# Weight rests moved from GpSimd to VectorE, a scaling moved from VectorE to ScalarE, and more PSUM banks for the output projection

## The chip, the cores and the metric

The kernel runs on one core of a Trainium2 chip. The core has TensorE (matrix products, results in PSUM), VectorE, ScalarE and GpSimd (elementwise work), and SyncE, which issues most of the transfers. Each engine works through its own instructions strictly in order and waits at semaphores for the others. The metric is the device time of one execution in microseconds (us); lower is better.

## The reference

One decoder layer over two token groups: a prompt of 512 tokens with 16 meta tokens ahead of it, and 64 sample tokens (8 sequences of 8). All is float32.

```python
u = rmsnorm(h, norm1_w)
z, xbc, dt_raw, q, k, v, qi, ki, wi, g_ssm, g_attn = split_in(u @ w_in)
y_ssm, ssm_new, conv_new = ssm_mixer(z, xbc, dt_raw, conv_prefix, h0, segments, ...)
y_att = attend(q, k, v, qi, wi, ki)        # indexer picks top-k keys, softmax over these
merged = sigmoid(g_ssm) * (y_ssm @ w_ssm_proj) + sigmoid(g_attn) * (y_att @ w_attn_proj)
h = h + merged @ w_out
u2 = rmsnorm(h, norm2_w)
h = h + square(relu(u2 @ w_up)) @ w_down
y = rmsnorm(h, final_norm_w)
```

The widths are 1024 for the model, 9320 for `w_in`, 2048 for the state-space branch and 4096 for the feed-forward part.

## The kernel before

**Three products for one.** Each large product in float32 precision is made of three on TensorE. An operand x is split into a head (x rounded to the fp32r format) and a rest (x minus its head); then head·head, head·rest and rest·head are added up in PSUM. For weights `weights` (L125) does this for each block of 128 x 1024 elements (512 KB): SyncE loads it into `wr` (2 buffers), ScalarE writes the head `wh` (L122), and GpSimd writes the rest `wl` by a subtraction (L123, in `split`). For `w_out` and `w_down` the two are called `dh` and `dl` (7 buffers each); for the others `wh` and `wl` (3 each). `wr` comes free for the next load when the rest is written. One first block has its rest on VectorE already. `split` also makes the rest `kL` of the indexer's keys, and `ysl` of the state-space outputs, which takes GpSimd and VectorE in turn.

**Stages, in order of time.** Norm and transposes; the indexer with its top-k (L420, L421 for the prompt, L529, L530 for the samples: a max and a replace in turn, on VectorE); the input projection, tile by tile (`mm3`, L145), whose tiles go through a convolution (`conv_tile`: L582 three times for one tile, then L587); the state-space scan (`states`, `chunk`), which is interleaved with the convolution by a small pipeline; the gates; the sample attention; the prompt's sparse attention (`query`) beside the projection of the state-space branch (L1039); the attention projection (L145 again, then L1072, L1073 and L1076 on VectorE); the output projection (`add_product`, L1164, called at L1185); and the feed-forward part in eight steps (`up` for w_up, `add_product` for w_down).

**In the scan** a chunk masks eight heads on VectorE (L733, tile `bc`) and feeds each to TensorE (L734). GpSimd weighs inputs (L665, L645), scales states (L678, L759), adds (L762, L766, L767) and takes powers (L155); L775 then writes a diagonal `rd` on VectorE for TensorE (L778).

**In the prompt's attention** `query` computes scores on TensorE, adds the mask with VectorE (L975), takes the exponential on ScalarE (L978), divides by the sum by means of a VectorE multiplication in place (L989, tile `P2`), and transposes on TensorE (L995).

**In the output projection** each `add_product` makes two halves of 512 columns; each half takes one PSUM bank of the tag "s" (3 banks), gets 8 or 12 products, and is added to `h2` by VectorE (L1178). Tag "a" has 3 banks too (used by `up` and, in turn with tag "w", by the transposes of the second norm); tag "w" has 2.

**What sets the order.** The program is written without engine queues: a scheduler works out the order of each engine's instructions ahead of time from dependencies, free buffers and its own cost figures. So a change of engine moves other instructions too. At run time the order of each engine is fixed.

Of the kernel before, what the change touches and what calls it, by code (L numbers as in the profile page):

```python
# [9 lines left out]
FT = mybir.dt.float32  # L10
# [3 lines left out]
AF = mybir.ActivationFunctionType  # L14
OP = mybir.AluOpType
# [55 lines left out]
def body(ctx, tc, a, o):  # L71
    nc = tc.nc
    SB, PS, DR = bass.MemoryType.SB, bass.MemoryType.PSUM, bass.MemoryType.DRAM
    act, dve, pool, pe, sy = nc.scalar, nc.vector, nc.gpsimd, nc.tensor, nc.sync
# [9 lines left out]
    def pst(tag):  # L84
        return psp.tile([128, 512], FT, tag=tag, name=tag, bufs=PSB[tag])
# [18 lines left out]
    def mis():  # L104
        alt[0] += 1
        return pst("as"[alt[0] % 2])

    def flat(t):
        return t.rearrange("p a b -> p (a b)")
# [10 lines left out]

    def split(raw, hi, lo, lo_eng=None):
        act.activation(hi, raw, AF.Copy)  # L122
        (lo_eng or pool).tensor_tensor(lo, raw, hi.bitcast(FT), op=OP.subtract)  # L123

    def weights(parts, at=None, lo_eng=None):  # L125
        raw = wp.tile([128, 8, 128], FT, tag="wr", name="wr", bufs=WB[0])
        lo, hi = [(at[0] if at else wp).tile([128, 8, 128], FR, tag=n, name=n, bufs=at[2] if at else WB[1])
                  for n in (at[1] if at else ("wl", "wh"))]
        for sel, src in parts:
            sy.dma_start(sel(raw), src)  # L130
        split(raw, hi, lo, lo_eng)
        return hi, lo
# [65 lines left out]
    for t in range(5):  # L198
# [7 lines left out]
        for q in range(2):  # L206
            ps = mis()
            pv = ps.rearrange("p (k n) -> p k n", k=4)
            for i in range(4):
                k = 4 * q + i  # L210
# [9 lines left out]
    ps = mis()  # L220
# [4 lines left out]
    ps = mis()  # L225
# [4 lines left out]
    for q in range(2):  # L230
        ps = mis()
# [23 lines left out]
    def inproj(parts, n=HT, w=None):  # L255
        w = w or weights(parts)
        out = []
        for h in range(2):
            ps = pst("w")
            mm3(ps, w, uh, ul, h * n, h * n + n)  # L260
            out.append(ps)
        return out

    def in_cols(c0):
        return [(lambda r: r, block(w_in, 0, c0))]
# [22 lines left out]
    with tc.tile_pool(name="p1", bufs=1) as p1:  # L288
# [11 lines left out]
        ps = mis()  # L300
# [4 lines left out]
        ps = mis()  # L305
# [10 lines left out]
        for ct in range(4):  # L316
            ps = inproj(in_cols(C_QI + 128 * ct) if ct else None, n=HQ, w=None if ct else wq0)
# [7 lines left out]
        kS = p1.tile([128, 528], FR, name="kS")  # L325
        kL = p1.tile([128, 528], FR, name="kL")
        split(kiT[:, 0:528], kS, kL)


# [15 lines left out]
        for t in range(4):  # L345
            L = LT[t]
            sc = am[:, LO[t]:LO[t] + L]
            for h in range(8):
                lq = qS[:, h, 128 * t:128 * t + 128]
                r = p1.tile([128, 528], FT, tag="ri", name="ri", bufs=2)  # L350
                for c0, c1 in pieces(L):
                    ps = mis()
# [20 lines left out]
        ps = mis()  # L373
# [34 lines left out]
        for c0, c1 in pieces(1032):  # L408
            ps = pst("a")
# [41 lines left out]
        ps = mis()  # L451
# [10 lines left out]
        ps = mis()  # L462
# [3 lines left out]
        ps = mis()  # L466
# [5 lines left out]
        ps = mis()  # L472
# [8 lines left out]
        ps = mis()  # L481
# [5 lines left out]
        ps = mis()  # L487
# [13 lines left out]
        for kt in range(6):  # L501
            c0, n = ((128 * kt, 128) if kt < 4 else (512, 16) if kt == 4 else (528, 64))
            ps = pst("s")
# [10 lines left out]
        for kp in range(8):  # L514
            hp, gi = divmod(kp, 4)
            parts = []
            for e in range(2):
                c0 = C_Q + 64 * (8 * hp + 4 * e + gi)
                parts.append((lambda r, e=e: r[:, :, 64 * e:64 * e + 64],
                              w_in[:, c0:c0 + 64].rearrange("(k p) c -> p k c", p=128)))  # L520
            ps = inproj(parts, n=HQ)
# [393 lines left out]
    with tc.tile_pool(name="p2h", bufs=1, reuse_waits="tile", side="right") as p2h, \  # L915
# [6 lines left out]
        for kv in range(4):  # L922
            hp, e = divmod(kv, 2)
# [13 lines left out]
        def query(t, hp, gp):  # L937

            L, nk = LT[t], t + 1
# [23 lines left out]
            cuts = [(0, L)] if L <= 512 else [(0, 400), (400, L)]  # L963
            PT = p2.tile([128, 2, 4, 2, 128], FT, tag="PT", name="PT", bufs=2)
            PR = p2.tile([96, 256], FR, tag="PR", name="PR", bufs=2)
            for g in range(2):
                P2 = p2q.tile([128, 2, 528], FT, tag="P", name="P2", bufs=3)
                mx = p2q.tile([128, 2, 6], FT, tag="mx", name="mx", bufs=4)
                for e in range(2):
                    lq = QS[:, 2 * gp + g, e, :]  # L970
                    for i, (c0, c1) in enumerate(cuts):
                        v = pst("s")[:, :c1 - c0]
                        pe.matmul(v, lq, KS[:, 2 * hp + e, c0:c1], start=True, stop=False)
                        pe.matmul(v, lq, KL[:, 2 * hp + e, c0:c1], start=False, stop=True)
                        dve.tensor_tensor_reduce(P2[:, e, c0:c1], v, at[:, c0:c1], 1.0, NEG, OP.add, OP.max,  # L975
                                                 accum_out=mx[:, e, i:i + 1])
                    dve.tensor_scalar(mx[:, e, 2:3], mx[:, e, 0:1], mx[:, e, len(cuts) - 1:len(cuts)], -0.125, op0=OP.max, op1=OP.mult)
                    act.activation(P2[:, e, :L], P2[:, e, :L], AF.Exp, scale=0.125, bias=mx[:, e, 2:3],  # L978
                                   accum_out=mx[:, e, 3:4])
                dve.reciprocal(mx[:, :, 4:5], mx[:, :, 3:4])  # L980
                tl = p2q.tile([128, 32], FT, tag="tl", name="tl", bufs=3)
                tv = tl.rearrange("p (e n) -> p e n", e=2)
                pool.tensor_tensor(tv, P2[:, :, 128 * nk:L], mx[:, :, 4:5].to_broadcast([128, 2, 16]), op=OP.mult)
                ts = p2q.tile([128, 3, 32], FR, tag="ts", name="ts", bufs=3)
                for i in range(2):
                    pool.tensor_copy(ts[:, i, :], tl)
                pool.tensor_tensor(ts[:, 2, :], tl, ts[:, 0, :].bitcast(FT), op=OP.subtract)
                for e in range(2):
                    dve.tensor_scalar(P2[:, e, :128 * nk], P2[:, e, :128 * nk], mx[:, e, 4:5], None, op0=OP.mult)  # L989
                yield  # L990
                for e in range(2):
                    ps = pst("a")
                    pv = ps.rearrange("p (k n) -> p k n", k=4)
                    for j in range(nk):
                        pe.transpose(pv[:, j, :], P2[:, e, 128 * j:128 * j + 128], idf)  # L995
                    (act.copy if e else dve.tensor_copy)(PT[:, e, :nk, g, :], pv[:, :nk, :])
                pr_ = pst("a")
                pe.transpose(pr_[:96, 0:128], flat(ts).bitcast(FT), idf)
                act.copy(PR[:, 128 * g:128 * g + 128], pr_[:96, 0:128])
# [11 lines left out]
            dve.tensor_tensor(yal[:, k0:k0 + 2, 128 * t:128 * t + 128], pv, h_.bitcast(FT), op=OP.subtract)  # L1011

        Pipe().run(query(t, hp, gp) for t in range(4) for hp in range(2) for gp in range(2))

    HALVES = ((0, HQ), (HQ, NQ))
    PARTS = ((0, 256), (256, NQ))
    w_s, w_a = a["w_ssm_proj"][0], a["w_attn_proj"][0]
    for q in range(4):
# [7 lines left out]
        for m in range(8):  # L1026
# [8 lines left out]
            for c0, c1 in HALVES:  # L1035
                ps = pst("w")
# [14 lines left out]
    mgh = p4a.tile([128, 8, NQ + NS], FR, name="mgh")  # L1051
    mgl = p4a.tile([128, 8, NP], FR, name="mgl")
# [5 lines left out]
    for m in range(8):  # L1058
# [9 lines left out]
        for c0, c1 in HALVES:  # L1068
            ps = pst("w")
# [19 lines left out]
    def row_weights(src, r0, n, at=(p4w, ("dl", "dh"), 7)):  # L1089

        return [[flat(x) for x in weights([(flat, src[r0 + 128 * k:r0 + 128 * k + 128, :])], at)] for k in range(n)]
# [25 lines left out]
    nb = [0]  # L1117

    def norm2(t):
        src, r = row_norm(t, t)  # L1120
        n = 128 if t < 4 else 64
        xn = p4.tile([128, D], FT, tag="jk", name="xn2", bufs=2)[:n]
        dve.scalar_tensor_tensor(xn, src, r, wrow[:n], op0=OP.mult, op1=OP.mult)
        if t == 4:
            pool.memset(h2[64:128, 4, :], 0.0)
        return lambda: turn2(t, xn, n)
# [34 lines left out]

    PIECES = ((0, 512), (512, 768), (768, 1024))

    def add_product(t, xh, xl, ws, cuts=((0, 512), (512, 1024))):  # L1164

        tok = slice(128 * t, 128 * t + 128)
        for c0, c1 in cuts:
            cc = slice(c0, c1)
            ps = pst("s")[:, :c1 - c0]
            for k, (wh, wl) in enumerate(ws):  # L1170
                if t < 4:
                    terms = (xh[k][:, tok], wh), (xl[k][:, tok], wh), (xh[k][:, tok], wl)
                else:
                    terms = (xh[k][:, tok], wh), (xh[k][:, tok], wl)
                for i, (x, w) in enumerate(terms):
                    pe.matmul(ps, x, w[:, cc], start=(k == 0 and i == 0),  # L1176
                              stop=(k == len(ws) - 1 and i == len(terms) - 1))
            dve.tensor_tensor(h2[:, t, cc], h2[:, t, cc], ps, op=OP.add)  # L1178
# [3 lines left out]
    for q in range(2):  # L1182
        ws = row_weights(a["w_out"][0], 512, 4) if q else wo
        for t in ORDER:
            add_product(t, [mgh[:, 4 * q + k, :] for k in range(4)], [mgl[:, 4 * q + k, :] for k in range(4)], ws)  # L1185
            if q == 1:
                turns.append(norm2(t))
                if t in (0, 1, 2):
                    turns.pop(0)()
# [40 lines left out]
    for s in range(8):  # L1230
        ws = [] if s < 7 else row_weights(a["w_down"][0], 512 * s, 4)
        nxt = ups(s + 1, ws) if s < 7 else None
        for i, t in enumerate(ORDER):
            add_product(t, *prev, ws, **({"cuts": PIECES} if s == 7 and i == 4 else {}))
            if s == 7 and i > 0:
                final(ORDER[i - 1])
        prev = nxt
# [26 lines left out]
```

## Time and profile before

| | |
|---|---|
| median of 3 runs | 1539.23 us (1535.28 to 1539.56) |
| the profiled execution | 1540.31 us |
| its span, first to last instruction | 1538.5 us |
| mean TensorE clock in it, share of full speed | 0.981 |

The profile gives for each engine the time in which it ran an instruction, as a share of the span, and for each group of instructions the count, busy time and mean. "Idle before, and its releaser" is the time the engine stood still just ahead of an instruction and what ended that. In a row of the view of waits, the engine on the left waited for the one on the right: total in us, how often, the longest. Rows of a timeline give the start in us, how long, engine, line, operation, output <- inputs. PE is TensorE's products, PEld its weight loads, DVE VectorE, ACT ScalarE, POOL GpSimd. Products overlap in TensorE's pipeline, so that a row of 0.30 us does not mean that the next one starts 0.30 us later.

### The profile page before, as it was taken

To read this page: it belongs to the slowest core of one execution; us is meant where nothing else is said; L and a number is where in the kernel's file an instruction comes from. 1 tells how busy PE (TensorE), PEld (TensorE's weight loads), DVE (VectorE), ACT (ScalarE), POOL (GpSimd) and SP (SyncE) were. 2 spreads that over 40 slices of the span, in tenths; PEclk is the share of its full clock that TensorE was granted. 3 is DMA by queue.
4 is the path that set the end of the run, shared out by engine and by line. 5 is a ranking of instruction groups with operands and counts; after the bars stand their busy time and mean duration, and the time that the engine had idled before them with its cause. 6 is when DMAs were issued, how large, how long until landed. Compare 5 with 4: busy or idle time off the path is not lost.

```text
span 1538.5 us, 26571 instructions
## 1 busy us (share of the span) xinstructions
PE 1456.4 (95%) x9960; PEld 1304.1 (85%) x9960; DVE 1008.7 (66%) x1905; ACT 667.8 (43%) x1484; POOL 713.8 (46%) x644
## 2 busy tenths in 40 slices
PE   6899999899998998999999999989998999999998
PEld 5888989898887987989678988888897998899886
DVE  5799999769769677363533788764565644564444
ACT  4454444555665654343645665522342321232211
POOL 2422353656666657465444964344154533352322
PEclk9999999999999999999999999999999999999999
DMA  6424645677886977766964532135233312332212
GB/s 173 115 56 107 171 141 149 204 232 204 231 238 169 261 209 208 210 180 202 339 218 145 154 90 80 33 119 183 58 98 108 110 55 69 96 95 68 71 41 69
DMA packets 297609, 221.55 MB, mean 144 GB/s; under 512 B 43820, under 2 KB 267360, under 8 KB 297456
## 3 DMA queue, kind: packets, MB, share of 16 engines
q1 hardware_dynamic: 292232, 200.98, 45.9%
q0 software_dynamic: 5248, 18.88, 3.6%
q8 instruction: 78, 1.28, 0.4%
q14 instruction: 51, 0.42, 0.1%
HBM read 174.97 MB, written 44.07 MB: 142 GB/s over the span
## 4 chain that ended last, share of the span: by engine, by line
PE 63%; DVE 16%; DMA 8%; issue 5%; ACT 4%; POOL 3%; SPq 2%; POOLq 0%; DVEq 0%; ACTq 0%
PE w L145 16%; PE s L1176 15%; PE a L145 10%; PE w L1039 7%; DVE ca L582 3%; PE s L871 2%; DVE bc L733 2%; DVE scs L530 2%; DMA bc<-d_ac 1%; DVE m8s L529 1%; ACT wh L122 1%; POOL wl L123 1%; DVE r L1200 1%; PE s L1005 1%; DMA wr<-in_w_up_dram 1%
## 5 line engine op out<-in xcount | busy, mean ns | idle before, releaser
L123 POOL TENSOR_TENSOR wl<-wr,wh 128x1024 fp32r<-128x1024 f32 x128 | 310.3, 2424 | 348.7 <-ACT wh L122 333.8
L145 PE MATMUL w<-uh,wh 128*128 128x288 f32 (+1 forms) x1168 | 359.6, 308 | 13.7 <-ACT rb L566 4.8
L145 PE MATMUL w<-ul,wh 128*128 128x288 f32 (+1 forms) x1168 | 358.0, 307 | 0.6 <-DVE ul L214 0.6
L145 PE MATMUL w<-uh,wl 128*128 128x288 f32 (+1 forms) x1168 | 356.3, 305 | 0.0
L145 PEld LDWEIGHTS w<-uh,wh 128*128 128x128 f32 x1168 | 226.3, 194 | 18.5 <-ACT rb L566 6.0
L145 PEld LDWEIGHTS w<-ul,wh 128*128 128x128 f32 x1168 | 226.2, 194 | 3.8 <-issue 2.3
L145 PEld LDWEIGHTS w<-uh,wl 128*128 128x128 f32 x1168 | 225.1, 193 | 2.9 <-issue 2.4
L122 ACT ACTIVATE wh<-wr 128x1024 fp32r<-128x1024 f32 x129 | 136.2, 1056 | 107.7 <-PE w L145 52.0
L123 POOL TENSOR_TENSOR dl<-wr,dh 128x1024 fp32r<-128x1024 f32 x40 | 99.1, 2480 | 157.9 <-ACT dh L122 157.9
L145 PE MATMUL a<-u2h,wh 128*128 128x288 f32 (+2 forms) x512 | 151.5, 296 | 1.0 <-ACT r L1199 1.0
L145 PE MATMUL a<-u2l,wh 128*128 128x288 f32 (+2 forms) x512 | 151.2, 296 | 0.0
L145 PE MATMUL a<-u2h,wl 128*128 128x288 f32 (+2 forms) x512 | 151.1, 295 | 0.0
L1178 DVE TENSOR_TENSOR h<-h,s 128x512 f32<-128x512 f32 (+1 forms) x101 | 67.1, 678 | 125.1 <-PE s L1176 124.5
L1176 PE MATMUL s<-dh,hh 128*128 128x512 f32 (+1 forms) x324 | 128.1, 396 | 6.2 <-DVE h L1178 6.2
L1176 PE MATMUL s<-dl,hh 128*128 128x512 f32 (+1 forms) x324 | 127.5, 395 | 0.0
L582 DVE SCALAR_TENSOR_TENSOR ca<-rb,cwT,ca 128x616 f32<-128x616 f32 x72 | 103.4, 1436 | 15.1 <-ACT ca L580 14.2
L1200 DVE TENSOR_TENSOR r<-r 128x288 f32<-128x288 f32 (+2 forms) x64 | 74.3, 1161 | 53.3 <-ACT r L1199 53.3
L122 ACT ACTIVATE dh<-wr 128x1024 fp32r<-128x1024 f32 x40 | 42.3, 1059 | 152.5 <-PE s L1176 131.2
L1176 PE MATMUL s<-dh,hl 128*128 128x512 f32 (+1 forms) x260 | 102.7, 395 | 0.0
L145 PEld LDWEIGHTS a<-u2h,wh 128*128 128x128 f32 x512 | 96.0, 188 | 2.1 <-ACT r L1199 1.5
L145 PEld LDWEIGHTS a<-u2l,wh 128*128 128x128 f32 x512 | 96.1, 188 | 0.7
L145 PEld LDWEIGHTS a<-u2h,wl 128*128 128x128 f32 x512 | 96.0, 188 | 0.0
(378 smaller groups left out, 3313.9 us busy)
## 6 DMA issues: line engine op xcount, KB each, us to landing
wr<-in_w_in_dram SPq DMA_DIRECT2D x64, 512.0 KB
wr<-in_w_up_dram SPq DMA_DIRECT2D x32, 512.0 KB
wr<-in_w_down_dram SPq DMA_DIRECT2D x32, 512.0 KB
st<-in_state_ssm_dram SPq DMA_DIRECT2D x16, 512.0 KB
bc<-d_ac SPq DMA_DIRECT2D x32, 256.0 KB
out_dram<-st SPq DMA_DIRECT2D x16, 512.0 KB
wr<-in_w_ssm_proj_dram SPq DMA_DIRECT2D x16, 512.0 KB
d_xd<-th SPq DMA_DIRECT2D x16, 296.0 KB
```

The source lines that it names most:

```text
L122: act.activation(hi, raw, AF.Copy)
L123: (lo_eng or pool).tensor_tensor(lo, raw, hi.bitcast(FT), op=OP.subtract)
L145: pe.matmul(ps[:, :c1 - c0], p[:, k, :], x[:, c0:c1], start=(k == 0 and i == 0), stop=(k == 7 and i == 2))
L529: dve.max(m8, scs)
L530: dve.match_replace(scs, m8, scs, MARK)
L582: dve.scalar_tensor_tensor(ca[:, 0:616], rb[:, k:k + 616], cwT[:, 24 * k + ct:24 * k + ct + 1], ca[:, 0:616], op0=OP.mult, op1=OP.add)
L733: dve.scalar_tensor_tensor(mt, mt, dts[:n, c, 8 * g + hh:8 * g + hh + 1], cb[:n, :n], op0=OP.mult, op1=OP.mult)
L871: pe.matmul(v[64 * hp:64 * hp + 64], QZ[:, hp, :], kk, start=True, stop=True)
L1039: pe.matmul(ps[:, :HQ], p[:, k, mc], x[k][:, c0:c1], start=(k == 0 and i == 0), stop=(k == 3 and i == 2))
L1176: pe.matmul(ps, x, w[:, cc], start=(k == 0 and i == 0), stop=(k == len(ws) - 1 and i == len(terms) - 1))
L1178: dve.tensor_tensor(h2[:, t, cc], h2[:, t, cc], ps, op=OP.add)
L1200: dve.tensor_tensor(r, r, r, op=OP.mult)
```

## The change

Three edits. The default engine of the subtraction in `split` becomes VectorE, which moves the rests of all weight blocks and of `kL`. The scaling of the prompt's probabilities goes to ScalarE as a copy with a scale per row. The output projection takes its PSUM banks in turn from the tags "s" and "a", six in all; `add_product` for w_down stays with "s".

```diff
     def split(raw, hi, lo, lo_eng=None):
         act.activation(hi, raw, AF.Copy)
-        (lo_eng or pool).tensor_tensor(lo, raw, hi.bitcast(FT), op=OP.subtract)
+        (lo_eng or dve).tensor_tensor(lo, raw, hi.bitcast(FT), op=OP.subtract)
...
                 for e in range(2):
-                    dve.tensor_scalar(P2[:, e, :128 * nk], P2[:, e, :128 * nk], mx[:, e, 4:5], None, op0=OP.mult)
+                    act.activation(P2[:, e, :128 * nk], P2[:, e, :128 * nk], AF.Copy, scale=mx[:, e, 4:5])
...
-    def add_product(t, xh, xl, ws, cuts=((0, 512), (512, 1024))):
+    def add_product(t, xh, xl, ws, cuts=((0, 512), (512, 1024)), banks="s"):
...
-            ps = pst("s")[:, :c1 - c0]
+            nb[0] += 1
+            ps = pst(banks[nb[0] % len(banks)])[:, :c1 - c0]
...
-            add_product(t, [mgh[:, 4 * q + k, :] for k in range(4)], [mgl[:, 4 * q + k, :] for k in range(4)], ws)
+            add_product(t, [mgh[:, 4 * q + k, :] for k in range(4)], [mgl[:, 4 * q + k, :] for k in range(4)], ws, banks="sa")
```

The lines behind L1168 move down by one. The order changes on all engines; three places show how.

GpSimd in the scan, second group of heads, third chunk of the prompt, before (xw, xb, hn, y, ss are tiles of the scan, rb of the convolution):

```order
L665 TENSOR_TENSOR xw<-xt,wdt 128x512
L645 TENSOR_TENSOR xb<-xb,wds 96x512
L759 TENSOR_TENSOR hn<-hn,elast 128x512
L563 MEMSET rb 128x3
L565 COPY rb<-scT 128x8x3
L155 TENSOR_TENSOR ss<-ss,cst 128x1
L123 TENSOR_TENSOR wl<-wr,wh 128x1024
L762 TENSOR_TENSOR y_5716<-y_5716,xd 128x512
```

The same place after the change:

```order
L665 TENSOR_TENSOR xw<-xt,wdt 128x512
L635 TENSOR_TENSOR xt_5858<-xt_5858,wdt 16x512
L759 TENSOR_TENSOR hn<-hn,elast 128x512
L645 TENSOR_TENSOR xb<-xb,wds 96x512
L762 TENSOR_TENSOR y_5716<-y_5716,xd 128x512
```

The weight's rest is gone from the run of GpSimd instructions; the scan's own have stayed, in a slightly other order.

VectorE in the scan, first group of heads, ahead of a chunk's masks, before:

```order
L728 TENSOR_TENSOR cb<-a,cst 128x128
L582 SCALAR_TENSOR_TENSOR ca<-rb,cwT,ca 128x616
L733 SCALAR_TENSOR_TENSOR bc<-bc,dts,cb 128x128 x8
L582 SCALAR_TENSOR_TENSOR ca<-rb,cwT,ca 128x616
L775 TENSOR_SCALAR rd<-cst,ss 128x128
```

The same chunk after the change:

```order
L728 TENSOR_TENSOR cb<-a,cst 128x128
L123 TENSOR_TENSOR wl<-wr,wh 128x1024
L733 SCALAR_TENSOR_TENSOR bc<-bc,dts,cb 128x128 x3
L587 SCALAR_TENSOR_TENSOR rb<-th,ca 128x528
L590 SCALAR_TENSOR_TENSOR rb<-th,ca 128x64
L733 SCALAR_TENSOR_TENSOR bc<-bc,dts,cb 128x128 x5
```

A weight's rest now stands in VectorE's queue ahead of the masks that TensorE waits for.

VectorE in the attention projection, in the fifth of its eight blocks, before (tga is the gate tile, mgl and mgh the rest and head of the merged activations):

```order
L1072 SCALAR_TENSOR_TENSOR tga<-tga,w 128x288
L1073 TENSOR_TENSOR tga<-tga,ms 128x288
L1076 SCALAR_TENSOR_TENSOR mgl<-tga,mgh 128x224
L1076 SCALAR_TENSOR_TENSOR mgh<-tga,mgh 128x64
L1072 SCALAR_TENSOR_TENSOR tga<-tga,w 128x288
```

The same place after the change:

```order
L1072 SCALAR_TENSOR_TENSOR tga<-tga,w 128x288
L123 TENSOR_TENSOR dl<-wr,dh 128x1024
L1073 TENSOR_TENSOR tga<-tga,ms 128x288
L123 TENSOR_TENSOR wl<-wr,wh 128x1024
L1076 SCALAR_TENSOR_TENSOR mgl<-tga,mgh 128x224
L1076 SCALAR_TENSOR_TENSOR mgh<-tga,mgh 128x64
L1072 SCALAR_TENSOR_TENSOR tga<-tga,w 128x288
```

The rests of `w_out` (dl) and of the projection's blocks (wl) now lie between the steps that free TensorE's banks.

## The prediction

> **What bounds the kernel now.** I read the page's first part, then the chain of waits, then the busy times by stage, then who TensorE waited for.
>
> ```profile
> PE 1456.4 (95%) x9960; PEld 1304.1 (85%) x9960; DVE 1008.7 (66%) x1905; ACT 667.8 (43%) x1484; POOL 713.8 (46%) x644
> ...
> PE 63%; DVE 16%; DMA 8%; issue 5%; ACT 4%; POOL 3%; SPq 2%; POOLq 0%; DVEq 0%; ACTq 0%
> ```
>
> TensorE is the bound: 95% busy, 63% of the chain. GpSimd, which does the work that is moved, holds only 3% of the chain, so its own 46% gives nothing by itself. The second place is VectorE, with 16%. The view by stretches shows where TensorE is not fed:
>
> ```profile
> 37.00:50.00 13.00, 9.20 (x50) 8.85 (x50) 11.57 (x14) 4.53 (x11) 10.27 (x9) 0.74 0.57 148
> 276.00:290.00 14.00, 10.19 (x65) 9.66 (x64) 13.97 (x19) 5.68 (x12) 7.52 (x7) 0.88 0.54 160
> 607.00:622.00 15.00, 8.04 (x45) 7.80 (x44) 10.30 (x6) 4.83 (x10) 12.13 (x10) 0.77 0.63 180
> 1030.00:1046.00 16.00, 11.01 (x67) 10.81 (x66) 9.14 (x9) 5.24 (x7) 7.54 (x4) 0.79 0.32 115
> 1163.00:1178.00 15.00, 10.03 (x36) 7.80 (x35) 8.71 (x11) 6.05 (x9) 9.56 (x4) 0.77 0.42 127
> ...
> 1200.00:1480.00 280.00, 279.08 (x1668) 252.47 (x1667) 149.98 (x166) 79.93 (x138) 107.55 (x44) 1.00 0.28 81
> ```
>
> After the length of the stretch stand PE, PEld, DVE, ACT and POOL busy, then the granted clock. In most of the feed-forward part (1200 to 1480) TensorE stands still for 0.9 of 280 us: nothing to gain there. The five short stretches each hold a hole of 4 to 7 us, and behind it a clock below 1. With half speed as the lower step, a mean clock of 0.79 over 16 us means 2 x 0.21 x 16 = 6.7 us at half speed, and a loss of half of that. The five hold 6.8 + 3.4 + 6.9 + 6.7 + 6.9 = 30.7 us at half speed, a loss of 15.4.
>
> Who ended TensorE's holes (total, count, longest):
>
> ```profile
> PE s L734 <- DVE bc L733: 9.8, 5, 4.2
> ...
> PE a L778 <- DVE rd L775: 7.0, 1, 7.0
> PE w L145 <- DVE tga L1072: 5.2, 2, 5.0
> ...
> PE a L602 <- DVE rb L587: 4.2, 4, 2.5
> PE w L145 <- DVE qS L322: 3.2, 1, 3.2
> ```
>
> and in the stretch from 1000 to 1172:
>
> ```profile
> PE s L1176 <- DVE h L1178: 7.1, 4, 5.0
> ```
>
> That is 36.5 us, all behind VectorE. The timeline says why VectorE was late (DVE and POOL rows of the same moments):
>
> ```profile
> 489.56 6.40 DVE L733 SCALAR_TENSOR_TENSOR bc<-bc,dts,cb 128x128 f32<-128x128 f32 x2
> 492.26 2.33 POOL L123 TENSOR_TENSOR wl<-wr,wh 128x1024 fp32r<-128x1024 f32 x1
> ...
> 608.23 6.89 DVE L775 TENSOR_SCALAR rd<-cst,ss 128x128 f32<-128x128 f32 x1 [1.57 <-POOL ss L155]
> 612.01 2.35 POOL L123 TENSOR_TENSOR wl<-wr,wh 128x1024 fp32r<-128x1024 f32 x1
> ...
> 1033.11 2.31 DVE L1076 SCALAR_TENSOR_TENSOR mgl<-tga,mgh 128x224 fp32r<-128x224 f32 x1 [4.34 <-ACT mgh L1074]
> 1035.35 2.35 DVE L1076 SCALAR_TENSOR_TENSOR mgh<-tga,mgh 128x64 fp32r<-128x64 f32 x1
> 1032.82 4.80 POOL L123 TENSOR_TENSOR dl<-wr,dh 128x1024 fp32r<-128x1024 f32 x2 [6.82 <-ACT dh L122]
> ...
> 1165.87 2.39 DVE L1203 TENSOR_TENSOR hl<-r,hh 128x288 fp32r<-128x288 f32 x1 [1.49 <-ACT hh L1201]
> 1168.18 2.59 DVE L1200 TENSOR_TENSOR r<-r 128x288 f32<-128x288 f32 x1
> 1165.58 2.36 POOL L123 TENSOR_TENSOR wl<-wr,wh 128x1024 fp32r<-128x1024 f32 x1 [2.92 <-ACT wh L122]
> ```
>
> A VectorE instruction that starts while GpSimd writes a rest ends with it: 64 columns take 2.35 us. This is common; three groups, first with their means, then with least, median and longest:
>
> ```profile
> L582 DVE SCALAR_TENSOR_TENSOR ca<-rb,cwT,ca 128x616 f32<-128x616 f32 x72 | 103.4, 1436 | 15.1 <-ACT ca L580 14.2
> ...
> L1200 DVE TENSOR_TENSOR r<-r 128x288 f32<-128x288 f32 x58 | 65.6, 1132 | 46.2 <-ACT r L1199 46.2
> L733 DVE SCALAR_TENSOR_TENSOR bc<-bc,dts,cb 128x128 f32<-128x128 f32 x128 | 62.9, 558 | 0.7 <-ACT xd L765 0.5
> ...
> L582 DVE SCALAR_TENSOR_TENSOR ca<-rb,cwT,ca x72: 834/918/3835, 193.3 to 573.8; 128x616 f32<-128x616 f32 x72
> ...
> L1200 DVE TENSOR_TENSOR r<-r x64: 425/455/2656, 1110.5 to 1479.2; 128x288 f32<-128x288 f32 x58, 128x256 f32<-128x256 f32 x3, 128x320 f32<-128x320 f32 x3
> ...
> L733 DVE SCALAR_TENSOR_TENSOR bc<-bc,dts,cb x160: 267/340/5339, 329.5 to 697.3; 128x128 f32<-128x128 f32 x128, 64x64 f32<-64x64 f32 x32
> ```
>
> Beyond what they need alone these spend (1436-834) x 72 = 43 us, (1132-455) x 58 = 39 and (558-340) x 128 = 28: 110 us.
>
> **The change part by part.** *The rests.*
>
> ```profile
> L123 POOL TENSOR_TENSOR wl<-wr,wh 128x1024 fp32r<-128x1024 f32 x128 | 310.3, 2424 | 348.7 <-ACT wh L122 333.8
> L123 POOL TENSOR_TENSOR dl<-wr,dh 128x1024 fp32r<-128x1024 f32 x40 | 99.1, 2480 | 157.9 <-ACT dh L122 157.9
> ...
> L123 DVE TENSOR_TENSOR wl<-wr,wh x1: 1220/1220/1220, 16.8 to 16.8; 128x1024 fp32r<-128x1024 f32 x1
> ```
>
> GpSimd loses 409 us. VectorE gets 168 x 1.22 = 205 us and gets back the 110 us above and what other groups wasted; so it grows by 95 us at most, with some 530 us idle now. A block's rest is also there 1.2 us sooner, and its load buffer free.
>
> What TensorE gains, hole by hole. Scan masks (9.8): other GpSimd work stands beside the rest, so I count the rest alone, 2.33 in each of the two long holes, 4.7; bounds 0 and 9.8. `rd` (7.0): likewise 2.35; bounds 0 and 7.0. Attention projection (5.2): 2.31 + 2.35 shrink to at most 0.455 each, the median of the wider L1200: 3.75. First product of the feed-forward part (5.0): 2.39 + 2.59 shrink the same way: 4.1. Convolution (4.2): I take 3. First stage (3.2): I take 2; both bounded by 0 and their rows. Sum 20 us. *The clock behind them*: at 37, 276, 1030 and 1163 the hole nearly closes, so 23.8 us at half speed go, worth 11.9; at 607 a hole of over 4 us stays and I count nothing. Sum 31.9.
>
> What it costs. VectorE is full in one stage, the top-k and first convolutions:
>
> ```profile
> 80.00:280.00 200.00, 192.06 (x1368) 181.61 (x1366) 196.64 (x370) 97.43 (x224) 74.61 (x67) 0.99 0.46 126
> 280.00:720.00 440.00, 411.20 (x3139) 372.94 (x3140) 300.75 (x520) 228.85 (x547) 267.61 (x252) 0.97 0.76 212
> 840.00:1000.00 160.00, 158.74 (x1157) 140.11 (x1154) 126.72 (x448) 95.12 (x255) 94.99 (x168) 1.00 0.32 92
> ...
> L123 POOL TENSOR_TENSOR wl<-wr,wh x25: 2359/2399/2812, 84.3 to 278.7; 128x1024 fp32r<-128x1024 f32 x25
> ```
>
> From 80 to 280 it is busy for 196.6 of 200 us, and 25 rests fall there: 25 x 1.22 = 30 us more, some 13 less in L582 (22 of its 72 lie there by start, so 22/72 of 43). The 17 left can slide: the sample top-k isn't needed before the sample attention, and in the new order 8 of its 32 rounds stand ahead of the first finished convolution tile, where 13 stood. From 280 to 720 VectorE has 139 us to spare. I take 5 us lost, of 0 to 17.
>
> The rest brings a wait onto VectorE too: it now waits for ScalarE's head, and so for the load, and behind it in the queue stand L733, L587 and L1073, for which TensorE waits. GpSimd's waits there were
>
> ```profile
> POOL wl L123 <- ACT wh L122: 67.8, 22, 5.5
> ```
>
> (280 to 720). How many of them held work that was ready, the row does not say, and the rests will stand among other work on VectorE. I take 4 us, of 0 to half of the 67.8.
>
> *The scaling.* Alone, ScalarE's copies bound it:
>
> ```profile
> L989 DVE TENSOR_SCALAR P<-P,mx x64: 274/434/1756, 858.6 to 988.2; 128x128 f32<-128x128 f32 x16, 128x256 f32<-128x256 f32 x16, 128x384 f32<-128x384 f32 x16, 128x512 f32<-128x512 f32 x16
> ...
> L723 ACT ACTIVATE bc<-bc 128x512 f32<-128x512 f32 x32 | 19.1, 620 | 0.1
> ```
>
> VectorE loses 64 x 0.434 = 28 us; ScalarE gains at most 64 x 0.62 = 40, and has 65 of 160 us free from 840 to 1000, where TensorE stands still for 1.3. Worth nothing; -1 to 3 as bounds, since the next exponential and the copies out of PSUM queue behind it on ScalarE.
>
> *The banks.* Of the 7.1 us at L1178 the 5.0 are counted above; 2.1 are left to gain, and the order now starts these products among the attention projection's, where they can fill holes but also wait for `dl`. I take 1, of -3 to 2.
>
> Sum: 31.9 + 1 - 5 - 4 = 24 us less than the profiled execution's 1540.3, so 1516.3; the median lies 1.1 below that execution, so 1515.
>
> **The rivals.** *A: VectorE stands at the head of its queue, slower.* If half of the 67.8 us, 34, reaches TensorE through L733 and L587, and five such holes each bring 3.4 us at half speed, the least of the stretches above (17 us, a loss of 8.5), the loss is 34 + 8.5 + 5 = 47 against a gain of 33: 1554. It decides from 33 us on. For it speaks that VectorE feeds TensorE directly, which GpSimd seldom does; against it, that a rest takes half as long and buffers turn round sooner.
>
> *B: the wait only changes sides, no change.* GpSimd keeps 300 us of work in the scan and attention, which read the same memory; a rest of 1.22 us on VectorE then holds back GpSimd, on whose results (L762, L767, L155) the chunks wait. If the scan's gains (4.7 + 2.35 + 3) go and each chunk of 20 loses 0.6 us, 12 us: 1515 + 10 + 12 = 1537. [...] Against B: 168 holds of 2.4 us become 168 of 1.2, and in the projections and the feed-forward part GpSimd has almost nothing left to exclude.
>
> *C: more goes than counted.* All 36.5 us of holes and the five half-speed stretches (15.4) go, with 4 lost: 48 us, 1540.3 - 48 - 1.1 = 1491.
>
> **How the numbers follow.** Forecast 0.55 (1503 to 1528 by its own bounds), C 0.15, B 0.14, A 0.16. A measurement here tells 0.3%, 4.6 us, from no change. Faster: 0.55 + 0.15 = 0.70; same: 0.14; slower: 0.16. The range takes in C and B with the edges of their bounds and leaves out A: 1486 to 1547.
>
> **What would show it.** Right: L1200's mean near 0.46, L582's near 0.9, no wait of 5 us at 1033 and 1166, a mean clock above 0.981, GpSimd near 300 us, VectorE at 950 to 1100. Wrong: rows in which VectorE's L123 waits for ScalarE's wh for tens of us while TensorE waits for L733 or L587; GpSimd's own groups (L762, L678) much longer than now; the stage of the top-k lasting longer by more than 5 us.

## The result and the profile after

The changed kernel takes 1494.76 us (median of 4 runs, 1492.77 to 1499.61) against 1539.34 us before: a ratio of 0.972, 95% interval 0.969 to 0.975, 44.6 us less. The profiled execution is the longest of the four, 1499.61 us, with a span of 1497.8 us.

Page, first part and chain of waits by engine:

```profile
PE 1443.2 (96%) x9960; PEld 1293.7 (86%) x9960; DVE 973.9 (65%) x2010; ACT 695.1 (46%) x1548; POOL 324.1 (22%) x475
...
PE 76%; DMA 11%; DVE 5%; ACT 2%; issue 2%; SPq 1%; POOL 1%; POOLq 0%; DVEq 0%; ACTq 0%
```

VectorE took over the rests of 168 weight blocks and is nevertheless busy for 34.8 us less than before. About half of that is the scaling, which went to ScalarE: with the rests alone (the first run below) VectorE is busy for 990.8 us, 17.9 less. Its share of the chain fell from 16% to 5%. TensorE stands still for 1497.8 - 1443.2 = 54.6 us of the span instead of 1538.5 - 1456.4 = 82.1. That is 27.5 of the 40.7 us by which the span shrank. The other 13.2 us are TensorE busy for less time with the same 9960 products, which is what a clock at half speed less often does: in the trace of before, the windows from 46 to 49 us read a granted clock of 0.50, and line 145's products of 288 columns start every 0.24 us there, where at 1.00 (1200 us) they start every 0.13. Read in windows of 2 us, TensorE's busy time at a granted clock below 0.9, times what was missing of full speed, comes to 22.9 us before and 9.4 after, 13.5 less; the lowest windows read 0.50 in both.

Where, by stage. The borders are landmarks of the program: the index scores' end, the input projection's last product, the last product of line 1039 (attention), the output projection's last product, the end. Busy us of PE, PEld, DVE, ACT and POOL, then clock, DMA share, GB/s. Before:

```profile
0.00:101.00 101.00, 79.28 (x522) 75.38 (x523) 72.06 (x158) 46.63 (x108) 33.46 (x28) 0.97 0.45 119
101.00:732.50 631.50, 595.69 (x4468) 548.01 (x4467) 477.56 (x830) 318.94 (x753) 345.73 (x321) 0.97 0.69 193
732.50:961.00 228.50, 226.72 (x1694) 187.65 (x1692) 145.58 (x469) 133.43 (x324) 126.89 (x174) 1.00 0.54 170
961.00:1104.00 143.00, 134.41 (x817) 116.00 (x816) 85.87 (x182) 47.67 (x89) 52.88 (x51) 0.98 0.33 102
1104.00:1538.50 434.50, 420.31 (x2468) 377.05 (x2466) 227.63 (x268) 121.08 (x211) 154.81 (x70) 0.99 0.27 79
```

After:

```profile
0.00:105.00 105.00, 84.21 (x560) 80.78 (x561) 71.77 (x181) 48.85 (x114) 11.51 (x18) 0.92 0.46 116
105.00:710.80 605.80, 583.07 (x4430) 533.42 (x4429) 477.59 (x881) 315.14 (x745) 208.31 (x256) 0.94 0.73 203
710.80:943.00 232.20, 229.28 (x1697) 189.68 (x1696) 147.35 (x437) 155.76 (x380) 88.94 (x162) 0.94 0.52 161
943.00:1075.50 132.50, 131.31 (x821) 115.08 (x820) 81.79 (x187) 54.21 (x101) 9.00 (x30) 0.95 0.36 110
1075.50:1497.80 422.30, 415.35 (x2460) 374.72 (x2459) 195.36 (x326) 121.13 (x209) 6.38 (x9) 0.99 0.27 82
```

The length of each row less its PE time is how long TensorE stood still:

| stage | length, before to after | predicted | measured | of it TensorE standing still |
|---|---|---|---|---|
| first stage | 101.0 to 105.0 | -5.4 | +4.0 | 21.7 to 20.8 |
| top-k, convolution, scan | 631.5 to 605.8 | -2.8 (holes -10.05, clock -1.7, costs +9) | -25.7 | 35.8 to 22.7 |
| attention | 228.5 to 232.2 | 0 | +3.7 | 1.8 to 2.9 |
| attention and output projections | 143.0 to 132.5 | -8.1 | -10.5 | 8.6 to 1.2 |
| feed-forward part | 434.5 to 422.3 | -7.6 | -12.2 | 14.2 to 7.0 |

The first border does not cut the work at the same place: 522 products lie ahead of it before, 560 after. By 105 us the kernel before had got through 550, so in work done the first stage did not get longer. The 38 products that moved across the border, some 5 us at 0.13 us each, make it look longer and the next stage shorter.

Who TensorE waits for after the change, from the top of that view:

```profile
PE s L211 <- DVE xn L205: 13.6, 4, 9.5
PE a L771 <- POOL xd L767: 4.6, 2, 3.1
PE a L676 <- DMA st<-in_state_ssm_dram: 4.3, 5, 1.7
PE w L145 <- DVE qS L322: 4.3, 1, 4.3
PE a L778 <- DVE rd L775: 4.0, 3, 3.1
```

The first is the kernel's start, and the same as before (13.6 us there too). The waits for the scan masks (9.8), for `tga` (5.2) and for `h` (8.4 in all) have left the list; `rd` is down from 7.0 to 4.0; the first stage's `qS` is not better (3.2, now 4.3).

VectorE's groups, mean ns behind the busy us, and for one of them the least, median and longest:

```profile
L123 DVE TENSOR_TENSOR wl<-wr,wh 128x1024 fp32r<-128x1024 f32 x129 | 161.1, 1249 | 117.1 <-ACT wh L122 114.9 <-PE s L863 1.3
L582 DVE SCALAR_TENSOR_TENSOR ca<-rb,cwT,ca 128x616 f32<-128x616 f32 x72 | 70.3, 977 | 0.4
L733 DVE SCALAR_TENSOR_TENSOR bc<-bc,dts,cb 128x128 f32<-128x128 f32 x128 | 42.7, 397 | 0.3
L1201 DVE TENSOR_TENSOR r<-r 128x288 f32<-128x288 f32 x58 | 25.9, 454 | 18.6 <-ACT r L1200 18.1
...
L1201 DVE TENSOR_TENSOR r<-r x64: 417/453/486, 1080.5 to 1439.1; 128x288 f32<-128x288 f32 x58, 128x256 f32<-128x256 f32 x3, 128x320 f32<-128x320 f32 x3
```

L1201 is the old L1200. Its mean fell from 1132 to 454 ns and its longest from 2656 to 486: in the feed-forward part, where GpSimd is now busy for 6.4 us, no instruction of this line is stretched any more. In the scan, where GpSimd keeps work of its own, L582 and L733 come down by a third, with single ones still stretched (the longest L582 takes 2.4 us).

### The profile page after: what moved, and what is told of

Read it like the earlier page. It is cut to its first block, busy times and chain, and to the rows that moved or that the text cites. A ratio compares the mean times of both kernels' runs of the same rounds, so it can differ in the third digit from the quotient of the medians.

```text
span 1497.8 us, 26553 instructions
## 1 busy us (share of the span) xinstructions
PE 1443.2 (96%) x9960; PEld 1293.7 (86%) x9960; DVE 973.9 (65%) x2010; ACT 695.1 (46%) x1548; POOL 324.1 (22%) x475
## 4 chain that ended last, share of the span: by engine, by line
PE 76%; DMA 11%; DVE 5%; ACT 2%; issue 2%; SPq 1%; POOL 1%; POOLq 0%; DVEq 0%; ACTq 0%
PE w L145 22%; PE s L1177 16%; PE a L145 14%; PE w L1039 7%; PE s L871 2%; PE a L1177 2%; PE s L1005 2%; DMA out_dram<-st 1%; DMA bc<-d_ac 1%; DMA wr<-in_w_ssm_proj_dram 1%; DMA st<-in_state_ssm_dram 1%; PE s L734 1%; PE a L894 1%; PE a L995 1%; DMA d_x<-tk 1%
## 5 line engine op out<-in xcount | busy, mean ns | idle before, releaser
L145 PE MATMUL w<-ul,wh 128*128 128x288 f32 (+1 forms) x1168 | 352.6, 302 | 0.6 <-DVE ul L214 0.6
L123 DVE TENSOR_TENSOR wl<-wr,wh 128x1024 fp32r<-128x1024 f32 x129 | 161.1, 1249 | 117.1 <-ACT wh L122 114.9
L1179 DVE TENSOR_TENSOR h<-h,s 128x512 f32<-128x512 f32 (+1 forms) x91 | 61.2, 679 | 100.4 <-PE s L1177 100.3
L155 POOL TENSOR_TENSOR rs<-rs,cst 128x1 f32<-128x1 f32 (+2 forms) x15 | 8.3, 552 | 446.0 <-DVE rs L154 445.9
L1039 PE MATMUL w<-ysh,wh 128*128 128x288 f32 x256 | 78.4, 308 | 0.2 <-DVE ms L1044 0.2
L123 DVE TENSOR_TENSOR dl<-wr,dh 128x1024 fp32r<-128x1024 f32 x40 | 49.0, 1225 | 45.3 <-ACT dh L122 45.2
```

Source lines behind the costliest of these rows:

```text
L123: (lo_eng or dve).tensor_tensor(lo, raw, hi.bitcast(FT), op=OP.subtract)
L145: pe.matmul(ps[:, :c1 - c0], p[:, k, :], x[:, c0:c1], start=(k == 0 and i == 0), stop=(k == 7 and i == 2))
L155: pool.tensor_tensor(dst, dst, K("half")[:p, :cols], op=OP.pow)
L1039: pe.matmul(ps[:, :HQ], p[:, k, mc], x[k][:, c0:c1], start=(k == 0 and i == 0), stop=(k == 3 and i == 2))
```

## The experiments

All times are medians, each with its ratio to the kernel before run beside it on the same chip (1536.3 to 1541.3 us).

**Each edit alone.** The default engine of `split` alone, the scaling alone, the banks alone: each is one piece of the diff above, put into the kernel before.

> The rests on VectorE alone, the other two edits left out. Theory (VectorE no longer stands behind GpSimd's rests): nearly the whole change, 1494 to 1502 us. Rival (the new order of instructions, or the other edits, made much of it): 1510 us or more.

> The scaling on ScalarE alone; rests on GpSimd, three banks. Theory: TensorE is full in that stage, so nothing: 1535 to 1543 us. Rival (VectorE was what bounds the prompt's attention): 1525 us or less. How far it lies from 1539 also shows what a new order alone is worth.

> The six banks alone; rests on GpSimd, scaling on VectorE. Theory: only some 2 us of waits at L1178 were left to gain: 1535 to 1541 us. Rival (the banks close the holes of the attention projection, of 5 us and what the clock adds, by letting the output products start early): 1525 to 1532 us.

Rests 1498.69 us, ratio 0.973 (0.970 to 0.976); scaling 1540.56, 1.001 (0.999 to 1.003); banks 1535.94, 0.998 (0.996 to 1.000). All three lie within what their theories said, and the rests carry all but a few us. But the stage of the two projections tells the parts apart. With the rests alone, its row and the only wait of TensorE that the view lists from 990 to 1110 us are

```profile
932.30:1074.70 142.40, 133.84 (x820) 115.58 (x819) 88.14 (x203) 47.80 (x89) 11.61 (x34) 0.98 0.35 105
...
PE s L1176 <- DVE h L1178: 6.4, 1, 6.4
```

The stage is as long as before (142.4 against 143.0): the wait for `tga`, 5.0 us long, is gone, and one of 6.4 us for the sum `h` that frees a bank of the output projection stands in its place. With the banks as well, neither is there and the stage takes 132.5 us (131.5 in the last run below, which has rests and banks without the scaling). The banks alone leave the `tga` wait as it was (5.3 us in two, 5.2 before), and the stage takes 145.1. So each edit closes one of two holes that stand in a row, and only both shorten the stage.

**What the rests did on GpSimd: reading or being busy.** Two kernels fill GpSimd again with work that nobody needs, VectorE keeping the rests. The first subtracts:

```diff
+    dmy = cp.tile([128, 192], FT, name="dmy")
...
         split(raw, hi, lo, lo_eng)
+        h2d = flat(hi).bitcast(FT)
+        for c in range(4):
+            hc = h2d[:, 192 * c:192 * c + 192]
+            pool.tensor_tensor(dmy, hc, hc, op=OP.subtract)
```

> The changed kernel, and for each weight block four subtractions of 128x192 on GpSimd (head minus itself, into a tile that nobody reads), some 2.4 us a block as the rests took before. Nothing else waits for them. Theory (exclusion while GpSimd reads): most of the gain is lost, 1525 to 1545 us, and L1200's mean is back above 0.8 us. Rival (rests that are ready sooner, load buffers that come free sooner): 1494 to 1503 us.

The second, with the same tile, only writes, but for one column:

```diff
...
         split(raw, hi, lo, lo_eng)
+        pool.tensor_copy(dmy[:, 0:1], flat(hi).bitcast(FT)[:, 0:1])
+        for _ in range(9):
+            pool.memset(dmy, 0.0)
```

> The changed kernel, with GpSimd filled again by work that hardly reads: per weight block one copy of a single column of the head and nine memsets of a 128x192 tile that nobody reads. If VectorE was held up because GpSimd was streaming two operands (the theory of the prediction), this costs little: 1493 to 1505 us, and L582's mean stays near 0.98 us. If what the rests cost on GpSimd was its queue (its own later work coming late), it costs as much as the four idle subtractions did or more: 1512 to 1530 us, with VectorE's durations as after.

1518.78 us, ratio 0.988 (0.984 to 0.992), and 1505.35 us, ratio 0.980 (0.978 to 0.982). The first lies between its theory (1525 to 1545) and its rival (1494 to 1503) and fits neither. GpSimd is busy for 811.6 us in the first and 785.0 in the second, about alike (713.8 before). GpSimd's main group and VectorE's group for `r` (L1201 after), with the subtractions:

```profile
L137 POOL TENSOR_TENSOR dmy<-wh 128x192 f32<-128x192 f32 x516 | 407.6, 790 | 386.6 <-ACT wh L122 359.5 <-ACT PT L1002 1.0
...
L1207 DVE TENSOR_TENSOR r<-r 128x288 f32<-128x288 f32 x58 | 36.5, 636 | 15.7 <-ACT r L1206 15.7
```

With the memsets:

```profile
L136 POOL MEMSET dmy<- 128x192 f32 x1521 | 394.0, 259 | 79.4
...
L587 DVE SCALAR_TENSOR_TENSOR ca<-rb,cwT,ca 128x616 f32<-128x616 f32 x72 | 67.3, 936 | 0.8 <-ACT ca L585 0.4
L1206 DVE TENSOR_TENSOR r<-r 128x288 f32<-128x288 f32 x58 | 25.9, 453 | 18.4 <-ACT r L1205 18.1
```

Beside a GpSimd that reads two operands VectorE's two-input `r` is stretched (636 ns in the mean), beside one that writes it is not (453, and 454 after). The 636 ns stay below the 800 that were expected; one subtraction here takes 0.79 us in the mean, where a rest took 2.42. The second kernel still gives back about 11 us, just beyond what the first theory allowed, although of the three VectorE groups only the scan's masks are longer (446 ns, 397 after): GpSimd being full costs something by itself here. Which of its results come late was not separated. One candidate is common to both: the head's buffer comes free later, and ScalarE waits for that, 8.1 us in the first and 8.9 in the second. So the first gives back 24 of the 44.6 us and the second 11; the 13 between them are what reading adds to being busy, and how the 20 that neither gives back divide is not shown. The rival, rests that are ready and load buffers that come free sooner, is not excluded for a part: in the trace of before the load queue waits for the rests of the blocks (310.1 us for `wl`, 159.1 for `dl`), and no other engine is listed as waiting for one, so it could act only by way of the loads.

**The length of one GpSimd instruction.** The rests go back to GpSimd, cut into quarters:

```diff
-        (lo_eng or dve).tensor_tensor(lo, raw, hi.bitcast(FT), op=OP.subtract)
+        if lo_eng or raw.shape[1] != 8:
+            (lo_eng or dve).tensor_tensor(lo, raw, hi.bitcast(FT), op=OP.subtract)
+        else:
+            for k in range(0, 8, 2):
+                pool.tensor_tensor(lo[:, k:k + 2], raw[:, k:k + 2], hi.bitcast(FT)[:, k:k + 2], op=OP.subtract)
```

> The changed kernel, with the rests back on GpSimd, but each in four subtractions of 128x256 instead of one of 128x1024. Theory 1, the length of one GpSimd instruction decides (VectorE can get in between two pieces): 1505 to 1525 us, and L1201's mean (the accumulation of the up and down projections, 0.45 us after and 1.13 us before) falls to 0.5 to 0.8 us. Theory 2, GpSimd's total busy time decides, however it is cut: 1530 to 1548 us, and that mean stays at about 1.1 us.

1521.61 us, ratio 0.991 (0.988 to 0.994): a third of the gain, with the rests of the blocks still on GpSimd. (The scaling and the banks are in this kernel; alone they measured 1.001 and 0.998.) Line 1205 here is the old L1200, line 586 the old L582, line 737 the old L733:

```profile
L127 POOL TENSOR_TENSOR wl<-wr,wh 128x256 fp32r<-128x256 f32 x512 | 403.2, 817 | 289.9 <-ACT wh L122 272.2 <-DMA Vg<-in_cache_v_dram,idx 8.6 <-PE a L149 4.2
...
L1205 DVE TENSOR_TENSOR r<-r 128x288 f32<-128x288 f32 x58 | 46.6, 804 | 64.7 <-ACT r L1204 64.3
L586 DVE SCALAR_TENSOR_TENSOR ca<-rb,cwT,ca 128x616 f32<-128x616 f32 x72 | 73.8, 1025 | 16.8 <-ACT ca L584 16.3
L737 DVE SCALAR_TENSOR_TENSOR bc<-bc,dts,cb 128x128 f32<-128x128 f32 x128 | 72.6, 632 | 0.3
```

The total on GpSimd rose (a quarter takes 0.82 us, not 2.42 / 4 = 0.61), and still VectorE's long groups gain (`r` 804 ns against 1132 before, line 582 1025 against 1436): length counts here, and not the total alone. But the short masks got longer than before (632 against 558 ns), perhaps as one may now meet several pieces, which was not shown, and `r` is at the edge of what the first theory said (804). Length decides in part.

**Where the rests pay.** VectorE takes them up to the end of the input projection and GpSimd afterwards, and the reverse:

```diff
-        (lo_eng or dve).tensor_tensor(lo, raw, hi.bitcast(FT), op=OP.subtract)
+        (lo_eng or rest_eng[0]).tensor_tensor(lo, raw, hi.bitcast(FT), op=OP.subtract)
...
+    rest_eng[0] = pool
```

> The changed kernel, but with VectorE taking the rests only up to the end of the scan and its input projection, and GpSimd again from the scan's output projection on. The landmarks of the two traces put about 22 to 29 us of the gain there, so 1512 to 1520 us. By the prediction's own terms (scan masks 4.7, the read of states 2.35, the convolution 3, the first stage 2, and about a third of the clock's 11.9) it would be 16 us, so 1522 to 1527 us.

> The complement: GpSimd takes the rests up to the end of the scan and its input projection, VectorE from there on. If the gains of the stages add up, its gain and that of the run before sum to the whole 44 us: 1515 to 1520 us. If the late stages only pass on what the early ones freed, the gain is below 10 us: 1529 us or more.

1518.59 us, ratio 0.988 (0.986 to 0.990), and 1523.77 us, ratio 0.993 (0.990 to 0.995). The early half alone brings more than the prediction's own terms had for it (1522 to 1527). The late half lies between its two expectations. The two ratios take off 1.2% and 0.75%, together less than the 2.8% of the whole change, so the medians do not add up; the profiled spans nearly do (21.4 and 17.0 against 40.7). These runs do not settle the difference.

**What a rest costs VectorE.** Each rest is subtracted twice into the same tile:

```diff
-        (lo_eng or dve).tensor_tensor(lo, raw, hi.bitcast(FT), op=OP.subtract)
+        for _ in range(1 if lo_eng else 2):
+            (lo_eng or dve).tensor_tensor(lo, raw, hi.bitcast(FT), op=OP.subtract)
```

> The changed kernel, with every weight block's rest subtracted twice on VectorE into the same tile (the second result is the same as the first), which adds 169 subtractions of 1.24 us, 210 us of VectorE's time, and lets the rest come 1.24 us later. It prices VectorE's share of the work by itself. If a rest on VectorE costs what the stages of the changed kernel that got longer show (about 8 us in the first stage and in the sampled attention together) the second set costs about the same: 1500 to 1512 us. If VectorE is close to being the bound once the rests are there, the part from 105 to 340 us, where it is busy 217.5 of 235 us, alone gets some 25 us longer: 1518 to 1545 us. If VectorE has room everywhere: below 1500 us.

1558.12 us, ratio 1.012 (1.010 to 1.014): 63 us more than after, slower than the kernel before, and above all three expectations. The expectation that VectorE is close to being the bound had put the loss before 340 us. None is there: by then TensorE had got through 2266 products, and 2269 after the change. From 340 to 700 us it got through 2371, where after the change it got through 2640. From 105 to 475 us, with the second set and then after the change, and the sample top-k (line 530 here, 529 after) in both:

```profile
105.00:475.00 370.00, 344.22 (x2508) 318.73 (x2507) 347.30 (x571) 185.00 (x428) 107.74 (x130) 0.96 0.60 166
...
L530 DVE MAX8 m8s<-scs x32: 1217/1226/1234, 167.6 to 474.3; 128x8 f32<-128x1032 f32 x32
```

```profile
105.00:475.00 370.00, 358.49 (x2680) 330.12 (x2679) 330.82 (x590) 201.66 (x472) 115.18 (x153) 0.94 0.68 188
...
L529 DVE MAX8 m8s<-scs x32: 1218/1228/1236, 157.8 to 337.1; 128x8 f32<-128x1032 f32 x32
```

The top-k that could slide to 337 us at no visible cost now slides to 474, far into the scan; VectorE is busy for 94% of these 370 us instead of 89%, and TensorE gets through 2508 products instead of 2680. From 340 to 735 us its largest wait is for one of the scan's sums on GpSimd (4.6 us after the change):

```profile
PE a L772 <- POOL xd L768: 20.3, 7, 6.2
```

So the delay reaches TensorE by way of GpSimd too; the chain from the second set to this sum was not followed. In the feed-forward part, where VectorE's busy share goes from 46% to 62%, next to nothing happens: from 1131 to 1556 us the row has 2464 products in 425 us, as after has 2463 in 423.

```profile
1131.00:1556.00 425.00, 417.05 (x2464) 375.31 (x2462) 262.05 (x388) 122.67 (x209) 6.91 (x10) 1.00 0.27 81
...
1075.00:1498.00 423.00, 415.85 (x2463) 375.13 (x2461) 195.76 (x327) 121.13 (x209) 6.38 (x9) 0.99 0.27 81
```

Of the 58.5 us by which the span grew, 35.8 are there at the input projection's last product (746.6 us, 710.8 after), 13.6 come in the attention, 7.0 in the two projections and 2.1 in the feed-forward part. So the change is near an edge in the scan, the stages right behind it bear no second set either, and only the feed-forward part has room.

**More of the same.** The scan's three sums (lines 762, 766, 767) go to VectorE as well; then its products of lines 665 and 759 too; then the three sums with the scaling back on VectorE.

```diff
-            pool.tensor_tensor(yv, yv, xd[:, :, :n], op=OP.add)
+            dve.tensor_tensor(yv, yv, xd[:, :, :n], op=OP.add)
...
-                pool.tensor_tensor(h8(hn), h8(G.hT), bc8(elast[:, c, g8]), op=OP.mult)
+                dve.tensor_tensor(h8(hn), h8(G.hT), bc8(elast[:, c, g8]), op=OP.mult)
```

> The changed kernel, with the three sums per chunk of the scan (lines 762, 766 and 767) on VectorE instead of GpSimd; the longest wait of TensorE in the scan that names GpSimd, 4.6 us in two waits for xd of line 767, should go, and VectorE's own two-operand work meets 48 us less of GpSimd's. If what the rests did holds for these too: 1485 to 1493 us. If VectorE's queue is what the scan waits for by now: 1497 to 1510 us.

> The run before, with the scan's products of lines 665 and 759 on VectorE as well, so that GpSimd keeps only the states' scaling there (line 678). VectorE gains some 18 us of work in a stage in which it is busy 259 of 360 us. If GpSimd's reading still costs something: 3 to 6 us below the run before. If VectorE's queue decides: as much above it.

> The changed kernel with the three sums of the scan on VectorE (as in the run of that alone) and the scaling of the probabilities back on VectorE: rests and banks without the scaling. The scaling alone measured +2 us with an interval that holds 0. If it costs a little: 1490 to 1494 us. If VectorE's queue in the query part (from 820 to 960 us) needs the relief once the rests are there: 1495 to 1500 us.

1494.01 us, ratio 0.971 (0.968 to 0.973); 1510.80, 0.982 (0.979 to 0.984); 1497.91, 0.971 (0.968 to 0.973). The sums take away the wait for `xd` (4.6 us; 0.4 is left) and bring nothing that can be measured: the time falls between the two expectations. The two products cost 17 us more, where 3 to 6 either way had been expected. Taking the scaling back changes nothing beyond the noise. With the products moved, TensorE waits most, from 340 to 714 us, for the copies out of PSUM:

```profile
PE w L145 <- ACT tg L275: 6.7, 3, 3.8
PE w L145 <- ACT zl L275: 4.4, 3, 2.0
```

Why ScalarE is late there was not followed further. No version found is measurably faster than the change as it is.

## Why the prediction was right, and where its terms were off

The prediction was 1515 us with a range of 1486 to 1547; 1494.76 lies in the range and on the predicted side, 20 us below the forecast and nearer to rival C (1491). The forecast's own bounds, 1503 to 1528, missed it, and they do not follow from the bounds given for the single terms, which are far wider (the masks alone 0 to 9.8, the costs 0 to 51). So the direction and the mechanism were right, and the size was not: a gain of 24 us was forecast and 44.6 measured.

*VectorE is held up while GpSimd computes a rest, and TensorE with it.* Right, and for VectorE's instructions shown from both sides: the groups came down with the rests' move, `r` stretched again when GpSimd read two operands (636 ns), and did not when it wrote (453). How much of the time this carries is bounded and not shown: see the two fillings of GpSimd. Its signs came: L1200's mean near 0.46 (0.454), GpSimd near 300 us (324), VectorE at 950 to 1100 (974), no 5 us wait at 1033 and 1166. L582's 0.98 missed the 0.9. The mean clock above 0.981 came in three of the four executions (0.991 to 0.993); the profiled one shows 0.955, for the reason told at the end. In the attention projection the rows that took 2.3 us each now read

```profile
1004.61 0.39 DVE L1076 SCALAR_TENSOR_TENSOR mgl<-tga,mgh 128x224 fp32r<-128x224 f32 x1
1004.91 0.22 DVE L1076 SCALAR_TENSOR_TENSOR mgh<-tga,mgh 128x64 fp32r<-128x64 f32 x1
```

*The clock behind the holes, 11.9 us: mis-sized.* This is the largest error. The prediction looked at five stretches below full speed. Two of them lie in the stage of top-k and scan, of which it counted one, 1.7 us. The trace of before has five more there:

```profile
224.00:234.00 10.00, 7.86 (x47) 7.56 (x47) 9.90 (x15) 5.31 (x12) 2.90 (x5) 0.83 0.66 190
384.00:396.00 12.00, 8.08 (x35) 5.92 (x36) 9.69 (x16) 4.41 (x13) 6.36 (x8) 0.72 0.62 167
452.00:461.00 9.00, 7.11 (x40) 6.40 (x39) 5.88 (x7) 6.37 (x19) 7.20 (x9) 0.81 1.02 266
493.00:506.00 13.00, 9.79 (x46) 7.51 (x47) 10.66 (x18) 5.14 (x16) 6.53 (x8) 0.74 0.67 168
562.00:571.00 9.00, 7.08 (x38) 6.59 (x39) 6.50 (x7) 6.83 (x19) 7.75 (x9) 0.81 0.98 254
```

By the prediction's own formula, (1 - clock) x length, they lose 1.7 + 3.4 + 1.7 + 3.4 + 1.7 = 11.9 us, and the one at 607, for which it counted nothing, 3.5. The one at 452 follows a single wait of 1.9 us (the windows from 457 to 459 read 0.50), so here it did not take a hole of 4 us. After the change two stretches of that kind are left in this stage:

```profile
310.00:318.00 8.00, 6.27 (x37) 6.04 (x36) 6.34 (x10) 2.31 (x5) 1.90 (x1) 0.76 0.76 232
357.00:365.00 8.00, 5.55 (x30) 4.27 (x31) 5.47 (x14) 1.30 (x2) 4.39 (x5) 0.76 0.58 162
```

With the 1.7 at 276 that is some 17 us lost before, and at most 3.8 after (0.24 x 8 twice; the base of that record is itself lowered, see the end). The gain is 13 us or more, where 1.7 was forecast. TensorE's busy time in this stage fell by 12.6 us, but some 5 of these belong to the 38 products that moved across the border (4468 and 4430), so the busy time bears out 8 of the 13 here; over the whole kernel the two agree (13.5 and 13.2). Outside this stage the trace of after has two stretches at half speed that the one of before had not, one at 28 to 34 us in the first stage (0.50 from 30 to 32), and one in the attention:

```profile
712.00:720.00 8.00, 5.98 (x22) 3.21 (x23) 5.25 (x11) 3.89 (x8) 1.38 (x2) 0.76 0.77 246
```

*The holes in the scan, 10.05 us: right in size.* TensorE stood still for 13.1 us less in that stage, with whatever the rests cost inside that figure. By hole, the masks gave all of 9.8 where 4.7 was forecast, `rd` 3.0 (2.35) and the convolution 3.0 (3); against that, waits for the loads of the states grew from 0.2 to 4.3.

*The costs, 5 and 4 us: not found where they were put.* The sample top-k did slide, from 281.8 to 337.1 us, which the prediction named as a sign against itself; no wait of TensorE names it, and the cost there is nothing that can be seen. The doubled rests show where this stops being free. What the forecast had wrong besides is the first stage: 5.4 us shorter was forecast, and in work done it gained about 1 us, 10 products by 105 us, as the 4.3 us wait for `qS` and the half speed behind it (0.50 from 43 to 49 us) stayed. The attention got 3.7 us longer. Some 1.8 of it is the stretch at half speed above, behind a wait of 2.1 us for `KcT`. By the same landmarks the attention takes 225.9 us with the rests alone, 228.6 with the scaling alone and 229.7 with the banks alone (228.5 before), so no edit does it by itself; the rest of the cause is open.

*The projections, 8.1 us: near in size (10.5), by luck, and wrong in mechanism.* The prediction credited the rests with 7.1 and the banks with 1. With the rests alone the stage gained 0.6 us, because the hole only moved on to the output projection's first product. What comes late next behind this hole was not asked.

*The feed-forward part, 7.6 us: 12.2.* TensorE's 14.2 us of standing still went down to 7.0, and its busy time by 5.0.

*The scaling, 0.* Right: 1.001 (0.999 to 1.003). ScalarE's row for it, least, median and longest, shows the price that nobody waits for (64 x 0.556 = 36 us, of at most 40 forecast):

```profile
L989 ACT ACTIVATE P<-P,mx x64: 386/556/732, 834.4 to 968.5; 128x128 f32<-128x128 f32 x16, 128x256 f32<-128x256 f32 x16, 128x384 f32<-128x384 f32 x16, 128x512 f32<-128x512 f32 x16
```

*Rival A, VectorE at the head of its queue.* Its first half came: from 280 to 720 us VectorE waited for ScalarE's heads,

```profile
DVE wl L123 <- ACT wh L122: 49.6, 18, 9.5
```

but the second half did not: in the scan TensorE's waits for VectorE are 4.0 us for `rd`, 1.2 for `rb` and 0.8 for `ss`, and none for the masks. What VectorE waited was covered; by which work, no run separates. *Rival B, the wait changes sides.* GpSimd's sum of line 762, after and before:

```profile
L762 POOL TENSOR_TENSOR y<-y,xd 128x512 f32<-128x512 f32 x16 | 24.0, 1501 | 3.2 <-DVE y L752 3.1
...
L762 POOL TENSOR_TENSOR y<-y,xd 128x512 f32<-128x512 f32 x16 | 21.6, 1353 | 10.1 <-DVE y L752 10.1
```

It is held up by 0.15 us each, 2.4 in all; with lines 767 and 155 (0.4 and 1.4) it is 4.2, where B needed 12 in the scan's chunks. GpSimd's small copies of lines 571 and 572, which B did not name, grew by 0.18 and 0.20 us each, 9.1 us in 48: one of line 572 that starts 0.26 us into a rest on VectorE, at 497.35 us, takes 1.01 us and ends 0.04 us behind it, where the shortest takes 0.18. So B's effect is there, but TensorE's only listed wait for GpSimd is the 4.6 us for `xd`. *Rival C* gave about the measured time by other terms: 15.4 us of clock and 36.5 of holes, with 4 lost, against 13.2 us of busy time and 27.5 of standing still, net.

## What to carry to other kernels

Where VectorE's two-input instructions of one shape have a median far below their mean (line 1200 before: 455 against 1161 ns), look at what GpSimd reads at those moments: an engine with 3% of the chain of waits held up the one that fed TensorE. Count every stretch of lowered clock in a stage, not the ones that are easy to see: here a hole of 1.9 us was followed by 3.4 us at half speed. Before comparing stages, count the products in each, as a border can move against the work. When a hole closes, name the next one on the same path before booking the gain; here it took two edits to shorten one stage.

## What had not been expected of the hardware

The profiled execution after the change shows a granted clock of 0.95 as its base up to 1120 us, where the others show 1. The products did not go slower for it. From 400 to 700 us, after the change and then with the rests alone, the two rows are

```profile
400.00:700.00 300.00, 287.45 (x2262) 258.55 (x2262) 204.85 (x404) 161.15 (x389) 125.39 (x145) 0.95 0.81 225
```

```profile
400.00:700.00 300.00, 287.53 (x2253) 259.65 (x2252) 201.36 (x396) 158.37 (x382) 125.47 (x144) 0.99 0.82 227
```

with as many products in the same time at 0.95 as at 0.99. So in these runs a mean clock may be set beside another only where both come from half-speed stretches; this is why the clock after is read here from stretches and from TensorE's busy time.
